# Delta-rule stage of a two-block stack: where the loads of inverted blocks are issued, and when the block levels begin

## The chip, the cores and the metric

The kernel runs on one core of a Trainium2 chip. The metric is device microseconds of one execution. TensorE (PE in the profile) multiplies, VectorE is DVE, ScalarE is ACT, GpSimd is POOL, SyncE is SP. SP, ACT and POOL can issue DMAs; an engine's instructions are taken in the order of its program, DMA issues among them, and an instruction that waits for a semaphore holds what stands behind it on that engine.

## The reference, cut to what matters

The program is a whole small network on 256 tokens of width 1024: a first block (two SwiGLU layers around an mLSTM mixer) and a second block of two layers, a gated delta rule and a sliding-window attention, each followed by a convolution-gated MLP. The change touches the delta rule alone. Its heart, for chunks of 64 tokens and 16 heads:

```
m     = where(strict, einsum('bnhcd,bnhsd->bnhcs', k_beta, k) * decay, 0)
t_mat = triangular_solve(m + eye, eye, lower=True, unit_diagonal=True)   # an inverse for every head and chunk
u     = einsum('bnhcs,bnhse->bnhce', t_mat, v_beta)
w     = einsum('bnhcs,bnhsd->bnhcd', t_mat, k_beta * exp(gc)[..., None])
# then a scan over chunks, a norm, a gate silu(z), and the output product with w_out
```

## The kernel before, in words

**Products.** Every large product streams its weights: `load_half` (L158) issues one DMA of 512 KB from SP into a buffer `raw` (four of them, L163), ACT casts it in two pieces to `whi` (L171), DVE subtracts to get `wlo` (L173), and `mm3` (L247) does three matmuls per tile, the "triple" (L250 to L252). One half holds eight tiles, which is one projection of the delta rule (eight triples, 24 matmuls). There are five pairs of split buffers, so a half's cast waits for the end of the projection five before its own. `wtile` (L194) loads a half when the products three halves earlier are emitted (`LOOK = 3`).

**The delta rule (L719 to L1181).** The chunks are taken as 128 by 128 matrices, four for each of the eight key heads `q8` (32 in all). `stage1` builds them, `ustore` (L966) writes them to HBM as `ud`. `invert(hf)` (L991) reads the 32 by 32 diagonal blocks of four heads `q8` and inverts them on POOL by forward substitution (L1001, L1006, 31 rounds); POOL then copies the result (L1007) and stores it as `xyd[hf]` (L1008). The two inversions, `hf` 0 and 1, follow one another on POOL. `levels(q8)` (L1015) then builds the inverse of the 128 by 128 matrix from its blocks: it loads the matrix again as two tiles `u` (L1018), loads the inverted blocks into a tile `XY` with four DMAs of 32 KB (L1032), and multiplies level by level (L1046, L1056, L1059, L1070, L1075). `solve` and `outp` follow with the head's own products and norm, up to the transposes of L1135. `u`, `r32`, `r64`, the outputs and more share 55 buffers called `u1k`.

**The order.** A planner, `Weave`, decides in which order the instructions are emitted. Fillers (projections of v, q, z, then the output product `op_all`) are taken a triple at a time, and each advances the planner's clock by 0.32; chains (norms, `stage1`, `invert`, `levels`) are generators that yield a cost and a latency. `invert` yields until the planner's estimate of POOL's end (`fill.pool`, L1009) plus 6.0 (L1010), and then marks `("i", hf)`, on which `levels` of four heads wait. `levels(3)` to `levels(5)` wait besides for the end of the head three before. `levels` yields 3.0 between the loads of `XY` and its first product.

**What the compiler makes of it.** The emission order is a priority. The framework's scheduler places each engine's instructions by its own estimate of when their inputs are there, and inserts the semaphores. `after(first, then)` (L144) adds an edge that this scheduler keeps and that puts no wait on the chip. Two such edges stand here: the loads of `XY` are placed after the weight load emitted last (`lastw`, L1035), and the first product of a level is placed after the product emitted last (`lastmm`, L1048).

Of the kernel before, what the change touches and what calls it, by code (L numbers as in the profile page):

```python
# [120 lines left out]
def stack_kernel(ctx, tc, w, xt, cols, rows, gw, baw, rel, kc, kb, out):  # L121
    nc = tc.nc
# [12 lines left out]
    def ps_mm(tag=None):  # L135
        if tag is None:
            rot[0] += 1
            tag = "st" if rot[0] % 3 == 0 else "mm"
        return pp.tile([128, 512], F32, name=tag, tag=tag, bufs=2 if tag == "st" else 4)
# [4 lines left out]
    def after(first, then):  # L144
        tc.add_manual_dep(then.ins, first.ins.name,
                          mybir.DependencyInfo(mybir.DependencyClass.NoSync, mybir.DependencyReason.DATA),
                          reason="order")

    lastw, lastmm = [None], [None]
# [569 lines left out]
    with tc.tile_pool(name="gd", bufs=1) as gp, tc.tile_pool(name="gw", bufs=2) as gq:  # L719
        def unit():  # L720
            return gp.tile([128, SEQ], F32, name="u1k", tag="u1k", bufs=55)
# [24 lines left out]
        fill = Weave(pe=0.32, dve=0.14)  # L746
# [159 lines left out]
        def urows(g):  # L906
            t = ud[g // 16]
            return bass.AP(tensor=t.tensor, offset=t.offset + (g % 16) * UG, ap=[[128, 128], [UG, 2], [1, 128]])
# [82 lines left out]
        def invert(hf):  # L991
            p0 = 64 * hf
            pr = slice(p0, p0 + 64)
            X, Y = Z[pr, :, :, 0], Z[pr, :, :, 1]
            nc.gpsimd.dma_start(out=B[pr], in_=bass.AP(tensor=ud[hf].tensor, offset=ud[hf].offset,
                                                     ap=[[129 * 32, 64], [128, 32], [1, 32]]))
            first = None
            for i in range(31):
                n = 31 - i
                t = tmp[pr, 0:n * (i + 1)].rearrange("p (r j) -> p r j", r=n)  # L1000
                ins = P_.tensor_tensor(out=t, in0=X[:, i, 0:i + 1].unsqueeze(1).to_broadcast([64, n, i + 1]),  # L1001
                                 in1=B[pr, i, i + 1:32].unsqueeze(2).to_broadcast([64, n, i + 1]), op=ALU.mult)
                if first is None and lastinv[0] is not None:
                    after(lastinv[0], ins)
                first = ins
                P_.tensor_tensor(out=X[:, i + 1:32, 0:i + 1], in0=X[:, i + 1:32, 0:i + 1], in1=t, op=ALU.add)  # L1006
            lastinv[0] = P_.tensor_copy(Y, X.rearrange("p i j -> p j i"))  # L1007
            nc.gpsimd.dma_start(out=xyd[hf], in_=Z[pr].rearrange("p a b t -> p a (b t)"))  # L1008
            fill.pool = max(fill.pool, fill.now + 6.0) + INVERT_COST  # L1009
            yield 0.0, fill.pool + 6.0 - fill.now, 0.0  # L1010
            fill.mark("i", hf)

        turn = [0.0]
# [1 line left out]
        def levels(q8):  # L1015
            u = [unit(), unit()]
            for j in range(2):
                nc.sync.dma_start(out=u[j], in_=urows(4 * q8 + 2 * j))  # L1018
            t = max(fill.now, turn[0])
            turn[0] = t + 5.0  # L1020
            yield 0.0, t - fill.now, 0.0
            if q8 < 6:
                XY = xyt[q8 % 3]
            elif q8 == 6:
                XY = gp.tile([128, 4, 256], F32, name="XY", tag="B")
                P_.memset(XY, 0.0)
            else:
                XY = gp.tile([128, 2048], F32, name="XY", tag="Z")[:, 0:1024].rearrange("p (g c) -> p g c", g=4)
                P_.memset(XY, 0.0)
            src = xyd[q8 // 4]  # L1030
            for a in range(4):
                ins = nc.sync.dma_start(out=XY[32 * a:32 * a + 32, :, 64 * a:64 * a + 64], in_=bass.AP(  # L1032
                    tensor=src.tensor, offset=src.offset + (16 * (q8 % 4) + a) * 2048,
                    ap=[[64, 32], [4 * 2048, 4], [1, 64]]))
                after(lastw[0], ins)  # L1035
            xyv = XY.rearrange("p g (c t) -> p g c t", t=2)
            X, Y = xyv[:, :, :, 0], xyv[:, :, :, 1]
            yield 0.0, 3.0, 0.0
            def us(g, r0, nr, c0, ncl):
                return u[g // 2][r0:r0 + nr, (g % 2) * 128 + c0:(g % 2) * 128 + c0 + ncl]  # L1040

            r32 = unit()[:, 0:128].rearrange("p (g n) -> p g n", g=4)
            pr = ps_mm("mm")
            for b in (0, 64):
                for g in range(4):
                    ins = T_.matmul(pr[b + 32:b + 64, g * 32:g * 32 + 32], us(g, b, 32, b + 32, 32), X[b:b + 32, g, b:b + 32],  # L1046
                                    start=True, stop=True)
                    if b == 0 and g == 0:  # L1048
                        after(lastmm[0], ins)
            for b in (32, 96):  # L1050
                S.copy(r32[b:b + 32], pr[b:b + 32, 0:128].rearrange("p (g n) -> p g n", g=4))
            yield 0.5, 0.9, 0.0
            px = ps_mm("mm")
            for b in (0, 64):
                for g in range(4):
                    T_.matmul(px[b:b + 32, g * 32:g * 32 + 32], r32[b + 32:b + 64, g, :],  # L1056
                              Y[b + 32:b + 64, g, b + 32:b + 64], start=True, stop=True)
                for g in range(4 if b == 0 else 0):
                    T_.matmul(px[b + 32:b + 64, g * 32:g * 32 + 32], Y[b + 32:b + 64, g, b + 32:b + 64],  # L1059
                              r32[b + 32:b + 64, g, :], start=True, stop=True)  # L1060
            for b in (0, 64):
                V.tensor_copy(Y[b:b + 32, :, b + 32:b + 64], px[b:b + 32, 0:128].rearrange("p (g n) -> p g n", g=4))
                if b == 0:
                    V.tensor_copy(X[32:64, :, 0:32], px[32:64, 0:128].rearrange("p (g n) -> p g n", g=4))
            yield 1.0, 0.4, 0.8

            r64 = unit().rearrange("p (g n) -> p g n", g=4)
            pr = ps_mm("mm")
            for g in range(4):
                T_.matmul(pr[64:128, g * 64:g * 64 + 64], us(g, 0, 64, 64, 64), X[0:64, g, 0:64], start=True, stop=True)  # L1070
            S.copy(r64[64:128], pr[64:128, 0:256].rearrange("p (g n) -> p g n", g=4))
            yield 0.43, 0.7, 0.0
            px = ps_mm("mm")
            for g in range(4):
                T_.matmul(px[0:64, g * 64:g * 64 + 64], r64[64:128, g, :], Y[64:128, g, 64:128], start=True, stop=True)  # L1075
            V.tensor_copy(Y[0:64, :, 64:128], px[0:64, 0:256].rearrange("p (g n) -> p g n", g=4))
            yield 0.43, 0.4, 0.3
            yield from solve(q8, Y)

        def solve(q8, Y):  # L1080
            n21 = N21.pop(q8)
            pcs = [unit(), unit()]
            pc = [pcs[g // 2][:, (g % 2) * 128:(g % 2) * 128 + 128] for g in range(4)]
            fill.need(("v", 2 * q8))
            fill.need(("v", 2 * q8 + 1))
            pw = ps_mm("mm")
            for j in range(2):
                vh = 2 * q8 + j
                T_.matmul(pw[:, j * 128:j * 128 + 128], Y[:, 2 * j], Vn[:, 0, vh, :], start=True, stop=True)
                S.activation(out=pc[2 * j], in_=pw[:, j * 128:j * 128 + 128], func=AF.Copy,  # L1090
                             scale=cc[:, 0, vh:vh + 1])
            yield 0.43, 1.0, 0.0
            pw2 = ps_mm("mm")
            for j in range(2):
                T_.matmul(pw2[:, j * 128:j * 128 + 128], n21[:, j * 128:j * 128 + 128], pc[2 * j],
                          start=True, stop=True)
            V.tensor_tensor(out=Vn[:, 1, 2 * q8:2 * q8 + 2, :], in0=Vn[:, 1, 2 * q8:2 * q8 + 2, :],
                            in1=pw2[:, 0:256].rearrange("p (a b) -> p a b", a=2), op=ALU.subtract)
            yield 0.43, 0.4, 0.34
            pw3 = ps_mm("mm")  # L1100
            for j in range(2):
                vh = 2 * q8 + j
                T_.matmul(pw3[:, j * 128:j * 128 + 128], Y[:, 2 * j + 1], Vn[:, 1, vh, :], start=True, stop=True)
                S.activation(out=pc[2 * j + 1], in_=pw3[:, j * 128:j * 128 + 128], func=AF.Copy,
                             scale=cc[:, 1, vh:vh + 1])
            yield 0.43, 1.0, 0.0
            yield from outp(q8, pc)
# [352 lines left out]
```

## Time and profile before

| | us |
|---|---|
| median of 3 runs (1329.46 to 1331.79) | 1330.91 |
| the profiled execution | 1331.48 |
| its span, first to last instruction | 1329.7 |

The profiled execution lies 0.57 us above the median. Busy shares of the span: PE 97%, PEld (weight load, overlaps PE) 94%, DVE 71%, ACT 59%, POOL 9%. The granted clock of TensorE has two levels, 2.4 GHz (shown as 1.00) and 1.2 GHz (0.50); over the whole span it was 0.988 in the mean. The delta rule runs from about 547 to 861 us. In the tables below a wait is written in brackets behind the instruction that ended it: [5.16 <-DVE gy L760] says that the engine was idle for 5.16 us before this instruction and that a result of L760 on DVE ended the idle time.

### The profile page before, as it was taken

The page shows a single profiled execution, that of the slowest core. Times are in us where ns is not written, and L with a number is a line of the kernel's source. Part 1 is how long each engine was busy: PE and PEld are TensorE (multiplying, and loading weights), DVE is VectorE, ACT ScalarE, POOL GpSimd, SP SyncE. Part 2 cuts the span into 40 slices and gives each one's busy share as a digit, 9 for nine tenths or more (in the row PEclk, how much of TensorE's full clock was granted, in tenths as well). Part 3 has the DMA queues.
Part 4 walks back from the last instruction along what each step waited for, and adds up shares of the span by engine and source line. Part 5 has one row for each costly group of instructions (what it writes and reads, how often), then busy time and mean ns, then how long its engine had stood idle before and what let it go on. Part 6 is the DMA issues. An engine that isn't in the chain of part 4 may idle for free.

```text
span 1329.7 us, 27373 instructions
## 1 busy us (share of the span) xinstructions
PE 1290.5 (97%) x10665; PEld 1252.4 (94%) x10665; DVE 940.2 (71%) x1856; ACT 788.3 (59%) x1823; POOL 123.6 (9%) x191
## 2 busy tenths in 40 slices
PE   8999999999999999999998799999999999999997
PEld 8999999988999999899997798999999989999997
DVE  7866546776777754588885765798886686998851
ACT  6554445665765554466655555777765676776641
POOL 0000000000000000101879400001100000000000
PEclk9999999999999999999998799999999999999999
DMA  7755553542465655235364352368975532476540
GB/s 258 241 175 175 176 170 112 165 147 72 154 206 183 188 189 169 75 96 183 120 204 153 84 163 80 104 171 233 236 218 197 181 102 69 158 237 191 190 159 33
DMA packets 70306, 213.38 MB, mean 160 GB/s; under 512 B 12517, under 2 KB 19205, under 8 KB 70048
## 3 DMA queue, kind: packets, MB, share of 16 engines
q1 hardware_dynamic: 65264, 204.36, 48.5%
q0 software_dynamic: 2304, 5.43, 2.0%
q10 hardware_dynamic: 2608, 1.84, 0.4%
q8 instruction: 84, 1.38, 0.4%
q14 instruction: 46, 0.38, 0.1%
HBM read 207.00 MB, written 4.59 MB: 159 GB/s over the span
## 4 chain that ended last, share of the span: by engine, by line
PE 77%; POOL 7%; DVE 5%; DMA 4%; ACT 3%; issue 3%; SPq 0%; DVEq 0%; POOLq 0%; ACTq 0%
PE mm L250 12%; PE mm L252 12%; PE mm L251 12%; PE st L251 7%; PE st L252 7%; PE st L250 7%; POOL Z L1006 3%; POOL tmp L1001 3%; DMA raw<-in_w 2%; PE mm L268 2%; PE mm L270 2%; PE mm L272 2%; DVE wlo L173 2%; PE st L268 1%; PE st L272 1%
## 5 line engine op out<-in xcount | busy, mean ns | idle before, releaser
L171 ACT CAST whi<-raw 128x512 fp32r<-128x512 f32 x752 | 439.5, 617 | 332.3 <-PE mm L251 115.0
L173 DVE TENSOR_TENSOR wlo<-raw,whi 128x1024 fp32r<-128x1024 f32 (+1 forms) x377 | 462.6, 1228 | 138.6 <-ACT whi L171 131.2
L250 PE MATMUL mm<-xh,whi 128*128 128x256 f32 (+1 forms) x1040 | 295.2, 284 | 0.0
L252 PE MATMUL mm<-xh,wlo 128*128 128x256 f32 (+1 forms) x1040 | 294.5, 283 | 0.5 <-DVE wlo L173 0.5
L251 PE MATMUL mm<-xl,whi 128*128 128x256 f32 (+1 forms) x1040 | 294.1, 283 | 0.0
L250 PE MATMUL st<-xh,whi 128*128 128x256 f32 (+1 forms) x720 | 207.8, 289 | 1.1 <-DVE u1k L920 1.1
L251 PE MATMUL st<-xl,whi 128*128 128x256 f32 (+1 forms) x720 | 206.7, 287 | 0.0
L252 PE MATMUL st<-xh,wlo 128*128 128x256 f32 (+1 forms) x720 | 206.1, 286 | 0.1
L252 PEld LDWEIGHTS mm<-xh,wlo 128*128 128x128 f32 x1040 | 196.0, 188 | 0.9 <-DVE wlo L173 0.7
L251 PEld LDWEIGHTS mm<-xl,whi 128*128 128x128 f32 x1040 | 195.8, 188 | 0.7 <-DVE xl L380 0.6
L250 PEld LDWEIGHTS mm<-xh,whi 128*128 128x128 f32 x1040 | 196.0, 189 | 0.5 <-DVE fu L428 0.2
L250 PEld LDWEIGHTS st<-xh,whi 128*128 128x128 f32 x720 | 137.8, 191 | 2.8 <-DVE u1k L920 1.3
L252 PEld LDWEIGHTS st<-xh,wlo 128*128 128x128 f32 x720 | 137.9, 192 | 0.4 <-DVE wlo L173 0.3
L251 PEld LDWEIGHTS st<-xl,whi 128*128 128x128 f32 x720 | 137.7, 191 | 0.1
L250 PE MATMUL mm<-hh,whi 128*128 128x256 f32 (+1 forms) x352 | 99.5, 283 | 0.0
L251 PE MATMUL mm<-hl,whi 128*128 128x256 f32 (+1 forms) x352 | 99.4, 282 | 0.0
L252 PE MATMUL mm<-hh,wlo 128*128 128x256 f32 (+1 forms) x352 | 99.4, 282 | 0.0
L250 PEld LDWEIGHTS mm<-hh,whi 128*128 128x128 f32 x352 | 67.0, 190 | 0.0
L251 PEld LDWEIGHTS mm<-hl,whi 128*128 128x128 f32 x352 | 66.5, 189 | 0.0
L252 PEld LDWEIGHTS mm<-hh,wlo 128*128 128x128 f32 x352 | 66.5, 189 | 0.0
L439 DVE SCALAR_TENSOR_TENSOR fu<-mm,colt,fu 128x255 f32<-128x255 f32 x108 | 51.1, 477 | 13.1 <-ACT fu L436 12.9
L250 PE MATMUL st<-hh,whi 128*128 128x256 f32 (+1 forms) x176 | 49.7, 282 | 0.0
(487 smaller groups left out, 2685.9 us busy)
## 6 DMA issues: line engine op xcount, KB each, us to landing
raw<-in_w SPq DMA_DIRECT2D x377, 512.0 KB, 4.0
u1k<-ud SPq DMA_DIRECT2D x16, 128.0 KB, 3.8
Tb<-bvd POOLq DMA_DIRECT2D x16, 128.0 KB, 6.1
gx<-in_w SPq DMA_DIRECT2D x2, 512.0 KB, 5.5
ud<-u1k POOLq DMA_DIRECT2D x8, 128.0 KB, 3.1
ud<-u1k ACTq DMA_DIRECT2D x8, 128.0 KB, 2.5
xyd<-Z POOLq DMA_DIRECT2D x2, 512.0 KB, 4.2
XY<-xyd SPq DMA_DIRECT2D x32, 32.0 KB, 3.4
```

Source lines behind the costliest of these rows:

```text
L171: S.copy(hi[:, c[0]:c[1]], raw[:, c[0]:c[1]])
L173: V.tensor_tensor(out=lo[:, c[0]:c[1]], in0=raw[:, c[0]:c[1]], in1=hi[:, c[0]:c[1]].bitcast(F32), op=ALU.subtract)
L250: T_.matmul(ps, hi, xhh, start=first, stop=False)
L251: T_.matmul(ps, hi, xll, start=False, stop=False)
L252: lastmm[0] = T_.matmul(ps, lo, xhh, start=False, stop=last)
L268: T_.matmul(pss[j], wts[j][0], xhh, start=(k == 0), stop=False)
L270: T_.matmul(pss[j], wts[j][1], xhh, start=False, stop=False)
L272: T_.matmul(pss[j], wts[j][0], xll, start=False, stop=(k == kt - 1))
L439: V.scalar_tensor_tensor(out=t[:, d:], in0=ps[:, :T - d], scalar=wc(2 - d), in1=t[:, d:], op0=ALU.mult, op1=ALU.add)
L1001: ins = P_.tensor_tensor(out=t, in0=X[:, i, 0:i + 1].unsqueeze(1).to_broadcast([64, n, i + 1]), in1=B[pr, i, i + 1:32].unsqueeze(2).to_bro ...
L1006: P_.tensor_tensor(out=X[:, i + 1:32, 0:i + 1], in0=X[:, i + 1:32, 0:i + 1], in1=t, op=ALU.add)
```

## The change

The four DMAs that load the inverted blocks of a head are issued from ACT instead of SP. They keep the edge to the weight load emitted last, which now runs from an instruction on SP to one on ACT, and get a second edge, to the product emitted last on PE. The planner marks an inversion as done 2.0 later on its clock (8.0 instead of 6.0 behind POOL's estimated end).

```
             fill.pool = max(fill.pool, fill.now + 6.0) + INVERT_COST
-            yield 0.0, fill.pool + 6.0 - fill.now, 0.0
+            yield 0.0, fill.pool + 8.0 - fill.now, 0.0
             fill.mark("i", hf)
...
             for a in range(4):
-                ins = nc.sync.dma_start(out=XY[32 * a:32 * a + 32, :, 64 * a:64 * a + 64], in_=bass.AP(
+                ins = nc.scalar.dma_start(out=XY[32 * a:32 * a + 32, :, 64 * a:64 * a + 64], in_=bass.AP(
                     tensor=src.tensor, offset=src.offset + (16 * (q8 % 4) + a) * 2048,
                     ap=[[64, 32], [4 * 2048, 4], [1, 64]]))
                 after(lastw[0], ins)
+                after(lastmm[0], ins)
```

## Rows read from the trace of the kernel before

**Rows 1.** Page, busy time of each engine: us, share of the span, instructions.

```profile
PE 1290.5 (97%) x10665; PEld 1252.4 (94%) x10665; DVE 940.2 (71%) x1856; ACT 788.3 (59%) x1823; POOL 123.6 (9%) x191
```

**Rows 2.** Stretches: length, busy us (instructions) per engine, granted clock, DMA share, GB/s.

```profile
690.00:790.00 100.00, 86.84 (x802) 80.79 (x801) 67.59 (x170) 57.13 (x174) 45.32 (x67) 0.90 0.46 131
697.95:703.11 5.16, 0.00 (x1) 0.00 (x0) 0.99 (x3) 1.80 (x4) 4.31 (x11) 0.70 1.00 323
703.11:706.80 3.69, 3.69 (x17) 3.69 (x18) 2.30 (x5) 2.10 (x6) 3.38 (x5) 0.50 0.72 203
...
755.95:764.90 8.95, 8.95 (x70) 8.31 (x70) 1.33 (x5) 3.28 (x11) 0.00 (x0) 0.50 0.28 76
820.00:850.00 30.00, 26.37 (x203) 24.57 (x203) 17.41 (x53) 16.03 (x52) 0.00 (x0) 0.94 0.32 105
```

**Rows 3.** PE in order of time, 690 to 704: start, us, line, operation, [idle before].

```profile
691.52 0.44 PE L810 MATMUL ax<-kct,gy 128*128 128x128 f32 x2 [1.10 <-DVE gy L760]
...
692.73 0.28 PE L250 MATMUL st<-xh,whi 128*128 128x256 f32 x1
...
695.93 0.28 PE L250 MATMUL ax<-xh,whi 128*128 128x256 f32 x1
...
697.67 0.28 PE L250 MATMUL ax<-xh,whi 128*128 128x256 f32 x1
703.11 0.69 PE L810 MATMUL ax<-kct,gy 128*128 128x128 f32 x2 [5.16 <-DVE gy L760]
```

**Rows 4.** ACT in order of time, 692 to 702.

```profile
692.81 0.62 ACT L171 CAST whi<-raw 128x512 fp32r<-128x512 f32 x1 [0.19 <-PE st L251]
...
701.10 0.62 ACT L171 CAST whi<-raw 128x512 fp32r<-128x512 f32 x1 [5.29 <-DMA raw<-in_w]
```

**Rows 5.** SP's DMA issues in order of time, 682 to 775.

```profile
682.31 0.41 SPq L163 DMA_DIRECT2D raw<-in_w  x1
693.67 2.44 SPq L1032 DMA_DIRECT2D XY<-xyd  x4
696.21 0.38 SPq L1018 DMA_DIRECT2D u1k<-ud  x1
696.68 0.89 SPq L163 DMA_DIRECT2D raw<-in_w  x2
...
738.72 0.35 SPq L163 DMA_DIRECT2D raw<-in_w  x1
749.43 1.73 SPq L1032 DMA_DIRECT2D XY<-xyd  x4
751.27 0.37 SPq L163 DMA_DIRECT2D raw<-in_w  x1
751.75 0.90 SPq L1018 DMA_DIRECT2D u1k<-ud  x2
```

**Rows 6.** SP's waits, first 682 to 694, then 737 to 750: total, times, longest.

```profile
SPq L1032 <- DMA xyd<-Z: 10.3, 1, 10.3
...
SPq L1032 <- DMA xyd<-Z: 10.9, 1, 10.9
```

**Rows 7.** PE in order of time, 737 to 769, with the second stop.

```profile
739.60 0.33 PE L1135 MATMUL mm<-kct,u1k 128*128 128x128 f32 x1 [1.77 <-ACT u1k L1131]
...
755.95 0.39 PE L1046 MATMUL mm<-XY,u1k 32*32 32x32 f32 x4 [4.01 <-DMA u1k<-ud]
...
768.40 0.28 PE L250 MATMUL st<-u1k,whi 128*128 128x256 f32 x1
```

**Rows 8.** Chain of waits, 735 to 782: start, us, what.

```profile
745.20 4.18 DMA xyd<-Z
...
751.75 4.07 DMA u1k<-ud
```

**Rows 9.** DVE and ACT in order of time, 746 to 764.

```profile
746.62 1.22 DVE L173 TENSOR_TENSOR wlo<-raw,whi 128x1024 fp32r<-128x1024 f32 x1
...
763.79 0.62 ACT L171 CAST whi<-raw 128x512 fp32r<-128x512 f32 x1 [1.81 <-PE st L251]
```

**Rows 10.** PE: first products of the levels of head 0, and of head 4.

```profile
708.44 0.59 PE L1046 MATMUL mm<-XY,u1k 32*32 32x32 f32 x16
...
782.22 0.52 PE L1046 MATMUL mm<-XY,u1k 32*32 32x32 f32 x14
```

**Rows 11.** Lines L1032 and L967: issue ns min/median/max, landing after issue in us.

```profile
L1032 SPq DMA_DIRECT2D XY<-xyd x32: 302/423/1117, 693.7 to 770.2; - x32
DMA to landing us min/median/max: 1.7/3.4/5.1
...
L967 ACTq DMA_DIRECT2D ud<-u1k x8: 366/367/395, 644.6 to 666.1; - x8
...
DMA to landing us min/median/max: 1.8/2.7/4.5
```

More of the change, by code (lines that the diff above doesn't have):

```diff
@@ L1009, in invert @@
             fill.pool = max(fill.pool, fill.now + 6.0) + INVERT_COST
-            yield 0.0, fill.pool + 6.0 - fill.now, 0.0
+            yield 0.0, fill.pool + 8.0 - fill.now, 0.0
             fill.mark("i", hf)
@@ L1031, in levels @@
             for a in range(4):
-                ins = nc.sync.dma_start(out=XY[32 * a:32 * a + 32, :, 64 * a:64 * a + 64], in_=bass.AP(
+                ins = nc.scalar.dma_start(out=XY[32 * a:32 * a + 32, :, 64 * a:64 * a + 64], in_=bass.AP(
                     tensor=src.tensor, offset=src.offset + (16 * (q8 % 4) + a) * 2048,
@@ L1035, in levels @@
                 after(lastw[0], ins)
+                after(lastmm[0], ins)
             xyv = XY.rearrange("p g (c t) -> p g c t", t=2)
```

## The prediction

> **What bounds the kernel now.** The busy shares come first: PE is busy for 1290.5 of 1329.7 us [rows 1], so a change off PE counts only where it ends or begins a stop of PE. Next I cut the stage into stretches. Over the 100 us around the block levels (690 to 790) PE is busy for 86.84 us only, at a mean clock of 0.90, while ACT, with 57.13, and the DMA engines, at a share of 0.46, have room [rows 2]. So something holds PE there. PE in order of time shows what: one stop of 5.16 us before 703.11 [rows 3] and one of 4.01 before 755.95 [rows 7], each followed by a stretch at 1.2 GHz, 703.11 to 706.80 and 755.95 to 764.90, in which PE never rests [rows 2].
>
> Both stops lead to SP. The first: PE waits for L760, which stands behind ACT's cast at 701.10, and that cast waited 5.29 us for weights [rows 4]. The weights were issued at 696.68, and the load before them at 682.31; between the two, SP stood at the first load of inverted blocks until 693.67 [rows 5], for 10.3 us, because POOL's blocks had not yet landed in HBM [rows 6]. The second: SP stands for 10.9 us in the same way before 749.43 [rows 5, 6], and the two `u` tiles of head 3, which have nothing to do with it, go out behind that at 751.75 and land 4.07 us later [rows 8], when PE begins.
>
> **The change part by part.**
>
> *SP loses 32 issues and both holds.* After 682.31 the next weights go out as soon as a `raw` buffer is free; the cast at 692.81 already waits for a split buffer and not for a load [rows 4], so with weights at hand the next cast comes with the end of the projection at 695.9 [rows 3], five us earlier, and the 5.16 us go. The slow stretch behind it goes with the stop: 3.5 us at half rate, worth 1.75. At the second stop the weights of 751.27 must still wait for the subtraction that ends at 746.62 + 1.22 = 747.84 [rows 9]; the `u` tiles then go out at about 748.3 and land at 752.4, 0.4 us after PE gets there at 751.94. So 3.6 of the 4.0 us go. The 1.10 us stop at 690.4 left the clock at full rate: the two transposes and eight matmuls behind it take 1.21 us, from 691.52 to 692.73 [rows 3], while one matmul alone takes 0.21 in the slow stretch (17 in 3.69 us [rows 2]). So a rest of 0.4 should cost no rate, and I let the whole slow stretch go here too: 8.95 us at half rate, worth 4.4. Sum of what goes: 5.2 + 1.75 + 3.6 + 4.4 = 14.9 us. If the cover fails, that is if something else is as late as the held load, each stop comes back at its own price.
>
> *ACT gets 32 issues, and the same wait.* Where they land on ACT decides. The edges put no wait on the chip, they only place the loads. The load at 682.31 is the one emitted last before the block loads. By the cast order it feeds the half cast at 692.81, and that cast waits for the projection that ends at 692.6, so it is used five projections after that one. The product emitted last belongs to the half three before it, the second projection after 692.6: those begin at 692.73 and 695.93 [rows 3], so it is the one from 695.93. The planner's extra 2.0 is six triples more at 0.32, some 2.2 us of PE at the 0.355 us per triple of this stretch (24 matmuls and two transposes from 692.73 to 695.93 [rows 3], less the transposes). So ACT meets the loads of head 0 when PE is at about 699 to 701, with the stop gone, and the blocks have landed by 693.67 [rows 5]: 5 us of margin, no wait. Likewise for head 4: the load of 738.72 is cast at 763.79 behind the end of a projection [rows 9], three halves less brings the projection that begins at 768.40 [rows 7], 19 us behind the landing at 749.4 [rows 8], and still 4 us if all 14.9 us come off. Behind a block load on ACT stand the casts and the PSUM evacuations that PE needs within a projection; they would be held as SP's loads are now.
>
> *The issue time on ACT.* No row shows these loads on ACT. The nearest, stores from ACT, take 0.367 us each, and the loads on SP 0.423 [rows 11]: 32 of them are 11.7 to 13.5 us, in a stretch where ACT is 57% busy [rows 2]. The bounds in PE time are 0 and 13.5; I take 1.5, nearer the lower one, since four in a row are 1.5 us and ACT's work has to be late by more than its slack to reach PE.
>
> *Blocks that come later.* The first product of head 0, at 708.44 [rows 10], stands at least 3.0 of planner time, nine triples or 3.2 us of PE, behind the loads. From ACT the loads take 4 x 0.367 us of issue and 1.8 to 4.5, in the middle 2.7 us of landing [rows 11]: 3.3 to 6.0, in the middle 4.2. So PE may stand for 0.1 to 2.8 us at each of heads 0, 1 and 2, 0.3 to 8.4 in all; other heads' products between load and use shorten that, and the scheduler may place more fillers ahead, so the lower bound is 0. I take 1.5. Heads 4 to 7 use their blocks late for another reason (782.22 [rows 10], after `u` tiles), so nothing is added there.
>
> *Levels that begin 2.0 later.* While there are fillers, PE does other work meanwhile. At the end there are none: from 820 to 850 PE is busy for 26.37 of 30 us [rows 2]. The bounds are a loss of 2.0, and a gain of 1.8 if the stop at L1135 [rows 7] falls away because its head moves. I take a loss of 1.0.
>
> The Trainium skill, page "DMA: Bandwidth & Descriptors", section "Issuing engines are not separate DMA queues", speaks against the change: DMAs issued from SP, ACT and GpSimd share the same 16 DMA engines, and issuing from several saves only the issue time, which is usually small. By that rule alone SP would save some 13 us of issues that nobody waits for, and the time would stay. The rows disagree about the size, as what SP loses here is a hold of 10.3 and 10.9 us [rows 6].
>
> **The sum.** 14.9 - 1.5 - 1.5 - 1.0 = 10.9 us. From the profiled execution's own 1331.48 us that is 1320.6; the profiled run lies 0.6 above the median of the runs shown, which makes 1320.0. I predict 1320.5. Its own range, with the costs between 0 and about 9 and up to 1.8 of gain, is 1315 to 1326.
>
> **The rivals.**
>
> *Only the first stop goes.* The `u` tiles of head 3 may be late because they wait for a `u1k` buffer of head 0, whose levels now begin later. For: they stand behind the held load in SP's order, so the trace can't show when their buffer came free. Against: SP issued them at once when its turn came. Then 6.9 us go and the costs of 4.0 stay: 1328.6.
>
> *The stop moves to another transfer.* While PE stood in the first stop, the DMA engines were busy throughout, at 323 GB/s [rows 2]; if the weights are late for lack of transfer time, they stay late on any queue. Against: the share over 690 to 790 is 0.46, and the burst is what had been held back. Then the gain covers no more than its costs: 1331.
>
> *ACT is held instead of SP (slower).* The edges place by the scheduler's estimate; on SP that estimate was too early by 10.3 and 10.9 us [rows 6]. If ACT reaches the loads before the blocks have landed, its casts and evacuations stop. This decides from the point at which ACT gets there before 693.6 or 749.4. SP's hold cost PE half its length, as loads run ahead; ACT's work runs ahead by one projection, some 3.2 us, so a hold of 10.3 would stop PE for 7 us, with 3 to 4 more at 1.2 GHz: about 10.5 each, 21 in place of the 15 of now, and the time 1337. Against: the product edge, which gives 5 us of margin. In the same page's section "Anatomy of one DMA — SWDGE (gpsimd) path" the Trainium skill says that a DMA's semaphore wait takes place on the issuing sequencer before dispatch; SP's waits [rows 6] agree, and on ACT it would be the same. Nor can the product edge fail harmlessly: if it doesn't move the loads, this is the case that comes.
>
> **How the numbers follow.** What a measurement of this kernel can tell from no change is about 0.2%, 2.7 us. The forecast gets 0.60, the rival with one stop 0.17, the moved transfer 0.10, ACT held 0.13. Faster: 0.60 and most of the second, 0.73; same: 0.14; slower: 0.13. The range reaches from the ceiling (14.9 and 1.8 of gain, 1314) to where the moved transfer ends, 1331; outside it lie ACT held and a little of the rest.
>
> **What would show it.** Right: on SP no wait for xyd is left; a cast directly after 695.9; no stop of PE over 2 us between 695 and 760, with the clock at 1.00 there; ACT's block loads issued without a wait, the first at about 699 to 701, with PE's waits before L1046 under 2 us each; PE busy for about 95 of the 100 us from 690 on. Wrong: ACT idle for several us in front of its first block load, a stop at L1046 of more than 3 us with the clock at 0.50 behind it, or the end of the stage, 820 to 850, longer by what was won.

## The result, and the profile after

The changed kernel takes 1338.2 us (median of 5 runs, 1337.15 to 1340.78) against 1331.02 for the kernel before beside it: ratio 1.0059, 95% interval 1.0042 to 1.0076. It is slower, 7.2 us by the medians, and outside the predicted range.

The mechanism that was forecast works in the main. The first page line after, then the block loads (duration in ns, minimum, median, maximum; first and last start; landing in us), the longest waits of PE from 640 to 870 (total, times, longest), the first product of head 0, and the stretch from 690 to 790 as in [rows 2], all of the changed kernel. Lines behind the edit are one higher there: L1047 is L1046 of before.

```profile
PE 1297.9 (97%) x10665; PEld 1257.5 (94%) x10665; DVE 942.5 (71%) x1856; ACT 787.9 (59%) x1823; POOL 124.8 (9%) x191
```

```profile
L1032 ACTq DMA_DIRECT2D XY<-xyd x32: 309/325/815, 696.8 to 782.5; - x32
...
DMA to landing us min/median/max: 1.6/2.8/5.1
```

```profile
PE ax L810 <- DVE gy L760: 4.8, 2, 3.7
PE mm L1136 <- ACT u1k L1132: 3.8, 5, 1.8
```

```profile
701.39 0.41 PE L1047 MATMUL mm<-XY,u1k 32*32 32x32 f32 x8 [0.71 <-POOL Z L1006]
```

```profile
690.00:790.00 100.00, 90.03 (x846) 83.22 (x844) 69.43 (x166) 57.75 (x173) 44.67 (x67) 0.97 0.44 124
```

The stops of 5.16 and 4.01 us [rows 3, 7] are gone, the loads cost ACT less than they cost SP (0.325 against 0.423 us each [rows 11]), and head 0 begins at 701.39 where it began at 708.44 [rows 10]. What is left is one stop of 3.7 us, at 747.32, again at L810 behind L760; so PE is busy for 90.03 of the 100 us from 690 on, where about 95 were named as a sign, at a clock of 0.97. Yet the stage ends later.

To see where, single executions are laid over one another on a **common scale**: a "triple" is the three matmuls L250 to L252, and each trace is shifted so that its 1300th triple is at 665.0 (the changed kernel by +2.31, the kernel before by -0.75). The 1620th triple, the 36th of the product behind the delta rule, then marks the end of the stage. Five stretches of that scale, 665 to 700, 740, 785, 820 and the end, first of the kernel before, then after (length, busy us of PE, PEld, DVE, ACT, POOL, granted clock, DMA share, GB/s):

```profile
665.75:700.75 35.00, 31.03 (x258) 30.14 (x256) 27.56 (x42) 18.36 (x42) 25.88 (x36) 0.99 0.71 211
700.75:740.75 40.00, 35.87 (x373) 33.02 (x374) 27.89 (x67) 24.77 (x78) 36.08 (x51) 0.92 0.37 116
740.75:785.75 45.00, 39.86 (x322) 37.37 (x321) 30.13 (x87) 26.19 (x81) 5.33 (x7) 0.85 0.45 128
785.75:820.75 35.00, 34.78 (x398) 31.54 (x396) 20.57 (x61) 17.98 (x56) 0.00 (x0) 1.00 0.32 99
820.75:878.10 57.35, 53.72 (x431) 51.29 (x430) 44.05 (x114) 41.87 (x108) 2.19 (x4) 0.97 0.38 113
```

```profile
662.69:697.69 35.00, 33.91 (x284) 33.12 (x282) 30.55 (x46) 22.14 (x51) 25.99 (x29) 1.00 0.78 237
697.69:737.69 40.00, 37.14 (x377) 33.76 (x376) 26.96 (x62) 21.59 (x71) 35.52 (x56) 0.96 0.27 81
737.69:782.69 45.00, 39.86 (x340) 37.41 (x339) 31.82 (x87) 25.77 (x79) 8.04 (x10) 0.96 0.43 124
782.69:817.69 35.00, 30.50 (x285) 26.13 (x284) 14.80 (x39) 14.28 (x44) 0.00 (x0) 0.71 0.40 121
817.69:881.41 63.72, 60.06 (x500) 57.10 (x499) 48.63 (x133) 45.02 (x122) 2.18 (x4) 0.97 0.33 98
```

Read each line as a loss: length less PE's busy time is idle, and busy time times (1 - clock) is what the clock takes. Before, the first three stretches lose 4.3, 7.0 and 11.1 us, together 22.4; after, 1.1, 4.3 and 6.7, together 12.2. **So 10.2 us are won by 785.** The fourth stretch loses 0.2 before and 13.3 after (4.5 idle, and 30.50 x 0.29 = 8.8 of clock), the last 5.2 and 5.5. The stage is 6.4 us longer: 3.2 by these losses, and 3.2 in what is left, PE's busy time counted at full clock, which this account can't split.

What fills that fourth stretch is seen at its start: PE in order of time, changed kernel, where head 4 begins.

```profile
785.08 0.28 PE L250 MATMUL st<-u1k,whi 128*128 128x256 f32 x1
...
785.42 0.28 PE L250 MATMUL st<-u1k,whi 128*128 128x256 f32 x1
786.59 0.28 PE L1047 MATMUL mm<-XY,u1k 32*32 32x32 f32 x4 [0.89 <-issue]
786.79 0.39 PE L251 MATMUL st<-u1k,whi 128*128 128x256 f32 x1
```

The products (fillers) do run ahead: triple 1519 comes at 811.2 before and 790.7 after, on the common scale. But head 4 starts at 788.9 instead of 781.5. From 791 on there are no fillers left (the next, the second half of the output product, needs head 4), and four heads run their small products alone, at a clock of 0.71. Counted in PE's program, head 4's first product stands behind triple 1481 before and behind triple 1516 after.

### The profile page after: what moved, and what is told of

Its sections match the earlier page's. It is cut to its first block, busy times and chain, and to the rows that moved or that the text cites. A ratio compares the mean times of both kernels' runs of the same rounds, so it can differ in the third digit from the quotient of the medians.

```text
span 1336.0 us, 27362 instructions
## 1 busy us (share of the span) xinstructions
PE 1297.9 (97%) x10665; PEld 1257.5 (94%) x10665; DVE 942.5 (71%) x1856; ACT 787.9 (59%) x1823; POOL 124.8 (9%) x191
## 4 chain that ended last, share of the span: by engine, by line
PE 75%; DVE 9%; DMA 5%; POOL 4%; ACT 3%; issue 3%; SPq 0%; DVEq 0%; ACTq 0%; POOLq 0%
PE mm L250 12%; PE mm L252 11%; PE mm L251 11%; PE st L251 6%; PE st L250 6%; PE st L252 6%; DMA raw<-in_w 4%; DVE wlo L173 3%; POOL Z L1006 2%; PE mm L270 2%; PE mm L272 2%; PE mm L268 2%; POOL tmp L1001 2%; PE st L268 1%; PE st L272 1%
## 5 line engine op out<-in xcount | busy, mean ns | idle before, releaser
L250 PE MATMUL mm<-xh,whi 128*128 128x256 f32 (+1 forms) x1040 | 296.3, 285 | 2.1 <-DVE fu L439 2.1
L252 PE MATMUL mm<-xh,wlo 128*128 128x256 f32 (+1 forms) x1040 | 295.6, 284 | 0.0
L250 PE MATMUL st<-xh,whi 128*128 128x256 f32 (+1 forms) x720 | 205.5, 285 | 1.1 <-DVE u1k L920 1.1
L252 PE MATMUL st<-xh,wlo 128*128 128x256 f32 (+1 forms) x720 | 204.2, 284 | 0.3 <-DVE wlo L173 0.2
L250 PEld LDWEIGHTS mm<-xh,whi 128*128 128x128 f32 x1040 | 197.0, 190 | 2.5 <-ACT fu L436 2.2
L252 PEld LDWEIGHTS mm<-xh,wlo 128*128 128x128 f32 x1040 | 197.0, 189 | 0.4 <-DVE wlo L173 0.2
L250 PEld LDWEIGHTS st<-xh,whi 128*128 128x128 f32 x720 | 136.0, 189 | 2.7 <-DVE u1k L920 1.3
L252 PEld LDWEIGHTS st<-xh,wlo 128*128 128x128 f32 x720 | 136.0, 189 | 0.9 <-DVE wlo L173 0.7
L250 PE MATMUL mm<-hh,whi 128*128 128x256 f32 (+1 forms) x352 | 99.6, 283 | 0.0
L252 PE MATMUL mm<-hh,wlo 128*128 128x256 f32 (+1 forms) x352 | 99.5, 283 | 0.0
L250 PEld LDWEIGHTS mm<-hh,whi 128*128 128x128 f32 x352 | 67.1, 191 | 0.0
L252 PEld LDWEIGHTS mm<-hh,wlo 128*128 128x128 f32 x352 | 66.6, 189 | 0.0
L252 PE MATMUL st<-hh,wlo 128*128 128x256 f32 (+1 forms) x176 | 49.8, 283 | 0.0
```

Source lines behind the costliest of these rows:

```text
L250: T_.matmul(ps, hi, xhh, start=first, stop=False)
L252: lastmm[0] = T_.matmul(ps, lo, xhh, start=False, stop=last)
```

## The experiments

The expectations use the common scale and these counts. In the table, places are the number of triples ahead of the first product of head 3 and of head 4 in PE's program, counted in each trace; losses are worked out from one profiled execution each as above; the ratio is to the kernel before on the same chip.

| kernel | places 3, 4 | loss to 785 | 785 to 820 | behind 820 | median us | ratio, interval |
|---|---|---|---|---|---|---|
| before | 1442, 1481 | 22.4 | 0.2 | 5.2 | 1331.0 | |
| after | 1465, 1516 | 12.2 | 13.3 | 5.5 | 1338.2 | 1.0059, 1.0042 to 1.0076 |
| e1_queue6 | 1446, 1494 | 11.7 | 5.8 | 5.3 | 1331.3 | 0.9991, 0.9967 to 1.0015 |
| e2_sp_late8 | 1448, 1517 | 13.3 | 11.0 | 5.4 | 1338.6 | 1.0041, 1.0016 to 1.0065 |
| e3_queue10 | 1446, 1486 | 13.4 | 4.5 | 4.1 | 1330.2 | 0.9988, 0.9963 to 1.0012 |
| e4_second_early | 1446, 1468 | 22.7 | 0.5 | 0.0 | 1324.7 | 0.9930, 0.9901 to 0.9960 |
| e5_own_u | 1449, 1504 | 14.8 | 11.6 | 6.0 | 1335.3 | 1.0037, 1.0009 to 1.0065 |
| e6_sp_edge | 1445, 1499 | 16.4 | 6.0 | 5.0 | 1329.3 | 0.9986, 0.9962 to 1.0010 |
| e7_no_edge | 1439, 1490 | 18.8 | 5.9 | 3.3 | 1331.2 | 1.0010, 0.9989 to 1.0030 |
| e8_own_u_early | 1444, 1457 | 20.5 | 9.5 | 0.4 | 1333.3 | 1.0010, 0.9984 to 1.0036 |
| e9_first_late | 1465, 1504 | 13.1 | 7.7 | 4.9 | 1332.3 | 1.0005, 0.9982 to 1.0029 |
| e10_second_late | 1446, 1499 | 8.6 | 7.2 | 3.6 | 1330.6 | 1.0000, 0.9982 to 1.0018 |
| e11_sp_early | 1438, 1469 | 25.4 | 0.8 | 0.3 | 1328.9 | 0.9993, 0.9975 to 1.0010 |
| e12_second_4 | 1446, 1482 | 20.1 | 6.3 | 0.3 | 1330.8 | 1.0004, 0.9986 to 1.0023 |
| e13_u_pool | 1465, 1516 | 13.9 | 11.0 | 5.4 | 1338.6 | 1.0044, 1.0025 to 1.0062 |
| e14_early_u_pool | 1446, 1468 | 11.5 | 0.3 | 0.0 | 1324.5 | 0.9940, 0.9917 to 0.9962 |
| e15_second_early_again | 1446, 1468 | 21.3 | 0.5 | 0.0 | 1323.2 | 0.9932, 0.9906 to 0.9958 |
| e16_place4 | 1465, 1476 | 22.0 | 3.1 | 1.3 | 1337.1 | 1.0048, 1.0028 to 1.0068 |
| e17_place4to7 | 1465, 1476 | 23.2 | 12.2 | 0.7 | 1345.3 | 1.0107, 1.0079 to 1.0136 |
| e18_place34 | 1430, 1476 | 23.1 | 0.5 | 1.1 | 1329.0 | 0.9989, 0.9968 to 1.0009 |

**Which part of the change costs: the queue or the 2.0?** `e1_queue6` is the change with 6.0, `e2_sp_late8` the kernel before with 8.0, `e3_queue10` the change with 10.0.

```
e1  -  yield 0.0, fill.pool + 8.0 - fill.now, 0.0    +  ... + 6.0 ...   (from the changed kernel)
e2  -  yield 0.0, fill.pool + 6.0 - fill.now, 0.0    +  ... + 8.0 ...   (from the kernel before)
e3  -  yield 0.0, fill.pool + 8.0 - fill.now, 0.0    +  ... + 10.0 ...  (from the changed kernel)
```

> The change with 6.0 in place of 8.0: block loads on ACT behind the product edge, levels begun as before. Cover theory: the two stops go and give PE about 14 us, but that time goes to fillers, and what counts is how many filler triples are left behind the first product of head 4 (the fillers end at triple 1520, where the output product needs head 4). Here it stands behind triple 1494, before at 1481, in the change at 1516. Against before that is 14 us won and 13 triples of 0.355 us (4.6 us) of cover lost: about 1322 us, between 1318 and 1327. Issue theory (32 DMA issues on ACT, or blocks that land later from there, delay the heads): about as the change, 1335 to 1338 us. Later-begin theory (each us of planner time at the start of a level is a us of the time): 2 us less than the change, 1336 us.

> The kernel before with 8.0 in place of 6.0: block loads stay on SP, levels begin later. Cover theory: in PE's program head 4's first product stands behind triple 1517, with 3 filler triples left, and both holds of SP stay: 36 triples (12.8 us) of cover less than before, about 5 us more at 1.2 GHz, the holds a little shorter: about 1345 us, between 1338 and 1349. Issue theory: as before, 1331 us, since nothing moves to ACT. Later-begin theory: 1333 us.

> The change with 10.0 in place of 8.0. In PE's program the first product of head 0 comes 5 triples later than in the change, but that of head 4 stands behind triple 1486 instead of 1516, since the scheduler places it elsewhere. Cover theory: 30 triples more of cover than the change and no holds: about 1321 us, between 1316 and 1327. Later-begin theory: 2 us slower than the change, 1340 us. Issue theory: as the change, 1338 us.

The queue alone gives no time (e1, 1331.3). 8.0 costs with the loads on SP as well (e2). So the cost of issuing on ACT is out as the cause: it is there in e1 and e3, and not in e2. But 10.0 costs nothing that can be told, so it is not a price per us of delay either. The cover theory (the time goes by the fillers left behind head 4's first product) was too large in e1 and e3 and at the edge of its range in e2; the later-begin theory missed all three.

**Does the chain of heads set the end?** `e4_second_early` lets the second inversion's heads begin earlier.

```
-  yield 0.0, fill.pool + 8.0 - fill.now, 0.0
+  yield 0.0, fill.pool + (6.0 if hf == 0 else -6.0) - fill.now, 0.0
```

> The change with 6.0 for the first inversion and -6.0 for the second: heads 4 to 7 are emitted 12 to 14 of planner time earlier. In PE's program head 4 begins behind triple 1468, with 52 fillers left, and the last transposes of heads 4 to 7 stand at 1504, 1519, 1535 and 1542. Cover theory: 14 us won at the stops and the idle time at the end of the stage shortened: 1314 to 1319 us. If ACT now meets the block loads of head 4 before they have landed (749.4 us in the trace of before), ACT is held for the difference, some 3 us or less, and the time is a few us longer. Issue theory: 1335 to 1338 us.

1324.7, faster than both kernels, though short of the 1314 to 1319 expected.

**Do the shared `u1k` buffers or the held queue delay head 4?** `e5_own_u` is the change with buffers of their own for the `u` tiles; `e6_sp_edge` is the kernel before with the product edge added to SP's loads; `e7_no_edge` has the loads on ACT without that edge and with 6.0; `e8_own_u_early` is e5 with the second inversion at -9.0.

```
e5  -  u = [unit(), unit()]
    +  u = [gp.tile([128, SEQ], F32, name="lu", tag="lu", bufs=4) for _ in range(2)]   # and u1k: bufs=51
e6  +  after(lastmm[0], ins)     (only this; loads on SP, 6.0)
e7  -  ins = nc.sync.dma_start(out=XY[...], ...)   +  ins = nc.scalar.dma_start(...)   (only this)
e8  e5 and  + (6.0 if hf == 0 else -9.0)
```

> The change with the u tiles of the levels in four buffers of their own (51 instead of 55 left for the rest), all else as in the change. Chain theory: the stage ends some 37 us behind the last transposes of head 7, those come some 58 us behind the first product of head 4, and that one waits for the later of two things: the u tiles of head 4 and the last transposes of head 3. In the change the u tiles decide (landed 7 to 8 us behind the transposes of head 3, since SP issues them behind weight loads). With own buffers they are there early, head 4 begins behind the transposes of head 3: 6 to 8 us less than the change, 1330 to 1332 us. Rival (begin 2.0 later, or loads on ACT, cost by themselves): 1337 to 1339 us as the change.

> The kernel before with the product edge added: block loads stay on SP, levels begin as before. The edge puts them four weight loads further back in SP's program, so SP should no longer be held at them. Chain theory: as the queue-and-edge kernel with 6.0 (first product of head 4 behind triple 1499, there 1494): within 3 us of that kernel and of before, 1328 to 1333 us, though both stops of PE go. Issue theory in what is left of it (32 issues on ACT cost a few us): 3 to 5 us faster than that kernel, 1325 to 1327 us.

> Block loads on ACT without the product edge, levels begun as before (6.0). In ACT's program the first load of blocks stands four halves earlier, so ACT reaches it before the blocks have landed and is held there, and again at head 4's. PE-bound theory (a stop of PE is paid in full): stops of 5 to 8 us at each hold, with slow clock behind: 1336 to 1340 us. Chain theory: the holds stop PE, but what they take is filler time of which the end of the stage has some to spare; the heads go on as the blocks land: 1329 to 1334 us, though PE stops for longer than in the queue-and-edge kernel.

> The change with own buffers for u and 6.0 for the first inversion, -9.0 for the second. In PE's program head 4 begins behind triple 1457 and the last transposes of head 7 stand at 1521 instead of 1557. Chain theory: head 4 begins as soon as its blocks have landed and head 3 is through, some 10 us earlier than with -6.0 alone; the fillers then last to the end, and PE bounds the stage: 1314 to 1320 us. If ACT is held at head 4's blocks (they land at about 751 us), the gain is some 3 us less. Issue theory: no faster than the kernel with -6.0, 1325 us.

e5 and e8 missed. In e6 SP waits for `xyd` no longer than 0.5 us, and the time is not told apart from e1's: against the hold the queue need not be moved, the edge does it. PE's second stop stays in e6 all the same, at head 3's `u` tiles:

```profile
753.50 0.31 PE L1047 MATMUL mm<-XY,u1k 32*32 32x32 f32 x4 [4.40 <-DMA u1k<-ud]
```

e7 is the most telling: its waits (of ACT, then of PE, as total, times, longest) show the third rival of the prediction at the blocks of the first inversion; at those of the second ACT is not held.

```profile
ACT Vn L812 <- DMA xyd<-Z: 11.0, 1, 11.0
```

```profile
PE ax L810 <- DVE gy L760: 11.8, 3, 9.6
```

ACT is held 11.0 us and PE stops for 9.6, and the time is 1331.2, as in e1, where ACT is not held and PE's longest stop is 3.0. **A stop of PE of that size costs nothing here that these runs can tell** (the two intervals, up to 1.0015 and 1.0030, overlap). That fits products with slack, and the table agrees: e10 loses least ahead of 785 (8.6) and takes 1330.6, e4 loses 22.7 there and takes 1324.7. In e8 the heads are too early: they run without fillers between them (clock 0.50 over 785 to 800), and the products are left over at the end.

**Which 2.0, and is the queue needed for e4's gain?**

```
e9   + (8.0 if hf == 0 else 6.0)      (from the changed kernel)
e10  + (6.0 if hf == 0 else 8.0)      (from the changed kernel)
e11  + (6.0 if hf == 0 else -6.0)     (from the kernel before: loads on SP, no product edge)
e12  + (6.0 if hf == 0 else -4.0)     (from the changed kernel)
```

> The change with 8.0 behind the first inversion and 6.0 behind the second. In program order head 3's first product stands behind triple 1465 as in the changed kernel (1446 with 6.0 twice) and head 4's behind 1504 (1494 with 6.0 twice, 1516 in the changed kernel). If the loss comes from the heads of the first inversion (head 3 late, so head 4 late): 1335 to 1338 us. Rival, the loss comes from the heads of the second inversion alone: 1331 us as with 6.0 twice.

> The change with 6.0 behind the first inversion and 8.0 behind the second. Head 3's first product stands behind triple 1446, head 4's behind 1499. If the loss comes from the first inversion's heads: 1330 to 1333 us. Rival, the second inversion's 2.0: 1336 to 1338 us.

> The kernel before with the loads of the blocks left on SP, and -6.0 instead of 6.0 behind the second inversion. Chain theory: head 4's first product stands behind triple 1469 instead of 1481, so the end of the stage comes 3 to 4 us earlier although SP is held for the second store some 11 us or longer: 1326 to 1329 us. Rival, SP's wait is what costs and the queue has to be moved first: 1331 to 1337 us.

> The change with 6.0 behind the first inversion and -4.0 behind the second. Head 4's first product stands behind triple 1482, the last head's transposes behind 1554 (1542 with -6.0, where the products were left over at the end). Balance theory (the later of heads and products sets the end): 1323 to 1325 us, at or below the 1324.7 with -6.0. Rival, only head 4's start counts: 1326 to 1328 us, between -6.0 and 6.0.

Neither 2.0 alone costs anything that can be told; both together do. Nothing in the expectations foresaw that. e11, which has e4's -6.0 but neither the queue nor the product edge, lies within its interval of no change, and that interval, from 0.9975, lies above e4's, which ends at 0.9960. So most of e4's gain needs the queue or the edge; which of the two isn't settled. e12 missed both theories: its head 4 stands at 1482, one triple behind that of the kernel before, and its time is that kernel's.

**SP's queue once more, or the place in PE's program?** e9 and the changed kernel keep within 2 us of one another up to head 4. There the changed kernel's `u` loads go out 6.7 us later on the common scale, behind three weight loads that wait for buffers. SP's issues, and its longest wait, changed kernel:

```profile
769.10 12.87 SPq L163 DMA_DIRECT2D raw<-in_w  x3
782.07 5.50 SPq L1018 DMA_DIRECT2D u1k<-ud  x8
```

```profile
SPq L163 <- DVE u1k L391: 18.7, 2, 11.4
```

That looks like the cause. `e13_u_pool` takes these eight loads off SP; PE's program is unchanged at the heads' first products. e14 does the same in e4, and e15 is e4 again.

```
-  nc.sync.dma_start(out=u[j], in_=urows(4 * q8 + 2 * j))
+  (nc.sync if q8 < 4 else nc.gpsimd).dma_start(out=u[j], in_=urows(4 * q8 + 2 * j))
```

> The changed kernel, with the eight u loads of heads 4 to 7 issued from POOL, whose program is done by then, instead of SP, where in the changed kernel they stand behind three weight loads that wait for raw buffers. PE's program order at the heads' first products is the changed kernel's (1396, 1407, 1419, 1465, 1516, 1520, 1520, 1520). SP theory: the tiles of head 4 land before 783 us on the common scale (789.4 in the changed kernel), its first product comes with the last transposes of head 3 at 782 to 783, the stage ends 6 us earlier than in the changed kernel, and the time is 1331 to 1333 us. Rival, the place of head 4 in the program order alone sets it: head 4 at 788 or later, 1337 to 1339 us.

> The change with 6.0 and -6.0 (the fastest run so far) and the u loads of heads 4 to 7 on POOL. Its stage ended with products left over, not with the heads: 1323 to 1326 us by that, no gain. Rival, head 4 still waits for its u tiles (landed 773.2, first product 776.2): 1320 to 1322 us.

> The change with 6.0 and -6.0 once more, beside the other two on one chip: 1323 to 1326 us if its gain over the kernel before (ratio 0.993) is the kernel's; 1328 to 1331 us if most of it was one build's or one chip's.

It is not the cause. POOL's issues and PE in order of time, e13:

```profile
766.78 0.75 POOL L1018 DMA_DIRECT2D u1k<-ud  x1 [15.45 <-PE mm L1136]
767.81 5.04 POOL L1018 DMA_DIRECT2D u1k<-ud  x7 [0.28 <-PE mm L1076]
```

```profile
787.23 0.28 PE L252 MATMUL st<-u1k,wlo 128*128 128x256 f32 x1
787.34 0.28 PE L250 MATMUL st<-u1k,whi 128*128 128x256 f32 x1
787.54 0.31 PE L1047 MATMUL mm<-XY,u1k 32*32 32x32 f32 x4
```

On the common scale the first `u` load goes out 16.0 us earlier, at 768.4, and its tiles land by 771.9, its blocks by 765.6; yet its product begins at 787.54 (789.2 on the common scale), with products in front of it and no wait: PE has simply not come to it. The Trainium skill, page "PSUM — Partial Sum Buffer", section "Engine vs sequencer instructions", says that matmuls start and complete in program order; these rows agree. e15 repeats e4's gain; e14 adds nothing to it.

**The place alone.** The planner emits head 4's first product behind triple 1467 before and 1476 after; the framework's scheduler places it behind 1481 and 1516. `e16_place4` holds it at 1476 by edges to every product emitted later, on top of e13; `e17_place4to7` holds heads 4 to 7, `e18_place34` heads 3 and 4. The edges move the heads behind as well: heads 5 to 7, at 1520 in e13, stand at 1487, 1493 and 1506 in e16 and in e18, and at 1486, 1491 and 1496 in e17.

```
 def mm3(ps, wt, x, first, last):
-    T_.matmul(ps, hi, xhh, start=first, stop=False)
+    ins = T_.matmul(ps, hi, xhh, start=first, stop=False)
+    if headmm[0] is not None:
+        after(headmm[0], ins)
...
                         after(lastmm[0], ins)
+                        if q8 == 4:              # e17: q8 >= 4, e18: q8 in (3, 4)
+                            headmm[0] = ins
```

> e13_u_pool with one more set of edges: every product emitted behind head 4's first product is also placed behind it, so that PE's program has it where it is emitted, behind triple 1476, and not where the framework's scheduler puts it, behind 1516. Order theory: PE passes triple 1476 at 768 to 770 us on the common scale, the tiles of head 4 land at 766 to 772, so its first product comes by 777 (789.2 in e13_u_pool), the stage ends 6 to 10 us earlier, and the time is 1327 to 1332 us. Rival, head 4 waits for something else that also comes late: its first product stays behind 785, and the time at 1336 to 1339 us.

> The same with heads 4 to 7 all held at their emitted places (1476, 1486, 1491, 1496 instead of 1516, 1520, 1520, 1520). If the chain of heads sets the end: 1325 to 1330 us. Rival: the products are left over behind the heads as in e8_own_u_early, and the gain is 0 to 3 us against e16_place4.

> The same with heads 3 and 4 at their emitted places (1430 and 1476 instead of 1465 and 1516). Head 3 earlier makes its transposes earlier, which stand ahead of head 4's first product: 1326 to 1331 us, 0 to 2 us under e16_place4. Rival: PE stops at triple 1430 for head 3's tiles, whose loads land at 733.6 and 760.4 in e13_u_pool, for more than 5 us, and the time is above that of e16_place4.

e16 missed. PE in order of time, e16, where head 4 begins (L1140 are the transposes, L1049 the first product):

```profile
777.12 0.64 PE L1122 MATMUL mm<-u1k 128*128 128x128 f32 x2
782.43 1.25 PE L1140 MATMUL mm<-kct,u1k 128*128 128x128 f32 x4 [4.68 <-ACT u1k L1136]
783.61 0.42 PE L1049 MATMUL mm<-XY,u1k 32*32 32x32 f32 x4
```

Held at 1476, head 4 comes to stand right behind the last transposes of head 3, and those are late because head 3 itself stands at 1465 where it is emitted behind 1430. PE waits 4.68 us for it, and the loss moves from 785 to 820 (11.0, now 3.1) to ahead of 785 (13.9, now 22.0). With head 3 in its place as well, e18 is at 1329.0: its interval, 0.9968 to 1.0009, lies wholly below those of e13, 1.0025 to 1.0062, and of e16, 1.0028 to 1.0068. e18 and e13 differ in these edges alone, e18 and e16 in the place of head 3 alone (the first products of the other heads stand at the same triples). So **the places of the heads in PE's program are what the 7 us hang on**; the 2.0, the queue and the issue cost are the same in all three. What the edges move on the other engines with them isn't separated. PE's stops are no help here: e18 has one of 7.17 us, longer than any of e13's (3.4), and is faster.

```profile
746.73 0.48 PE L1140 MATMUL mm<-kct,u1k 128*128 128x128 f32 x1 [7.17 <-ACT u1k L1136]
```

No single place orders the times. Of the kernels without held fillers, those with head 4 at 1481 to 1499 take 1329.3 to 1331.3 us and those with it at 1516 or 1517 take 1338.2 to 1338.6; but e9 has head 3 as late as the changed kernel and takes 1332.3, e16 has head 4 early and takes 1337.1, and e17, with heads 3 and 4 where e16 has them, takes 1345.3. Nor does the start of head 4 tell it: on the common scale it comes at 782.4 in e18 and at 783.4 in e16, and the rest of the gain comes behind it, where from 785 to 800 e16 has a clock of 0.78 and e18 one of 1.00; e16, then e18:

```profile
785.24:800.24 15.00, 15.00 (x155) 13.47 (x154) 4.49 (x11) 4.18 (x12) 0.00 (x0) 0.78 0.20 54
783.10:798.10 15.00, 15.00 (x170) 13.27 (x164) 4.71 (x11) 4.42 (x13) 0.00 (x0) 1.00 0.45 129
```

The last three stretches of e18, then of e15 (columns as above):

```profile
738.10:783.10 45.00, 35.73 (x307) 32.73 (x307) 31.42 (x86) 25.00 (x79) 13.21 (x19) 0.80 0.39 116
783.10:818.10 35.00, 34.51 (x378) 31.22 (x372) 19.11 (x58) 17.80 (x57) 0.00 (x0) 1.00 0.39 116
818.10:873.48 55.38, 54.32 (x456) 52.50 (x456) 44.68 (x113) 42.15 (x106) 2.18 (x4) 1.00 0.44 122
```

```profile
739.05:784.05 45.00, 38.29 (x355) 35.06 (x355) 27.47 (x84) 24.60 (x84) 7.74 (x13) 0.85 0.38 105
784.05:819.05 35.00, 34.53 (x354) 31.94 (x354) 24.15 (x73) 22.01 (x69) 0.00 (x0) 1.00 0.43 130
819.05:871.26 52.21, 52.21 (x433) 50.50 (x433) 44.54 (x110) 40.96 (x104) 2.18 (x4) 1.00 0.45 129
```

In e15 PE is never idle from 819.05 to the end, at full clock, though it lost as much ahead of 785 as the kernel before: fillers last until the heads are done. e17, with fillers held behind all four heads, loses most of all.

## Why the prediction was wrong

*SP loses both holds, 14.9 us.* Right as to PE's stops, wrong as to the end. Both stops went, a new one of 3.7 us came at 747.32, and the losses to 785 fell by 10.2 us. That this lies near the 10.9 of the forecast is chance: 14.9 were to go, and the costs that make 10.9 of it mostly did not show there. **The step that failed is that a stop taken from PE comes off the end.** The prediction asked only what PE waits for there, and not whether the work behind the stop has slack. The products that it delayed now run 10 to 20 us ahead (triple 1480 at 769.9 instead of 780.4, 1519 at 790.7 instead of 811.2 on the common scale), and the end gains nothing by it: without the extra 2.0 the change takes 1331.3 (e1), as the kernel before, and e7 puts a 9.6 us stop back with no loss that can be told. In e1 the losses to 785 fall by 10.7 and those from 785 to 820 rise by 5.6, where head 4 stands 13 triples later than before; how much of the won time was slack, and how much that place took back, no run separates.

*Issue time on ACT, 1.5 (0 to 13.5).* Nothing that can be told: e6 on SP and e1 on ACT differ by 2.0 us, with overlapping intervals.

*Blocks that come later, 1.5.* Wrong sign, if anything: head 0's first product waited 0.71 us, and came 4.0 us earlier on the common scale (7.05 in the traces' own times [rows 10], less the shifts of 2.31 and 0.75).

*Levels that begin 2.0 later, 1.0 (-1.8 to 2.0).* Mis-sized, and the cause of the loss. I read the 2.0 as a delay on the clock. It moves the emission of heads 3 and 4 by 5 and 9 triples (1425 to 1430, 1467 to 1476); in PE's program the change moves them by 23 and 35 (1442 to 1465, 1481 to 1516). Of these 4 and 13 come with the queue and the edge (e1), whose emission is that of before; the scheduler turned the 2.0 into the other 19 and 22, and on SP into 6 and 36 (e2). With 6.0 the same change takes 1331.3, with 8.0 1338.2: some 7 us. The last of the signs named as "wrong", an end of the stage longer by what was won, came true, at 785 to 820 rather than at 820 to 850.

*The rivals.* "Only the first stop goes" did not happen in the change; in e6 the second stop did stay, where SP issues the `u` tiles at 747.35, behind a weight load that had waited 14.2 us for its buffer. "The stop moves to another transfer" did not happen: the new stop at 747.32 ends with a result of VectorE, and ACT waits for no load there. "ACT is held" did not happen in the change, and where it did, in e7, it did not cost the 10.5 us put on it; that its 1337 lies next to the measured 1338.2 is chance.

Left open: why the scheduler places head 4 so late with both 2.0 (1516 on ACT, 1517 on SP) and not with either one or with 10.0; its estimates leave no row in a trace. The account by stretches is of single executions: e14's has a stage of 197.5 us, 10 shorter than e15's, after 8.4 us more ahead of it, while the medians are 1.3 apart, which I can't explain. e1, e3, e10 and e11 have stages 3.1 to 5.8 us shorter than the kernel before and medians that are not told apart from it. The medians, not these stages, carry the conclusions.

## What to carry to other kernels

Before you price a stop of the busiest engine, ask what the work behind it is needed for: where independent work fills the engine between links of a chain, a stop that only delays the filler can be free, as the 9.6 us of e7 were as far as these runs can tell, and taking it away can leave the end of the chain with nothing to run beside it. Count what is left of the filler when the chain ends; the two should run out together. Where a scheduler stands between emission and program, compare the engine's program order before pricing any change of a due time, as here a move of 9 triples became one of 22, on SP of 36.

## What the runs showed of the hardware

Where the heads' small products run with no fillers between them, the granted clock falls although PE looks busy: in the changed kernel its mean is 0.71 over 35 us in which PE is busy for 30.50, and in e8 it is 0.50, which is 1.2 GHz, over 15 us in which PE never rests:

```profile
783.95:798.95 15.00, 15.00 (x125) 13.03 (x123) 7.49 (x22) 6.18 (x22) 0.00 (x0) 0.50 0.23 71
```

Executions of the same instructions can differ in steps: PE's program is the same in all twenty kernels up to triple 1300, yet from triple 600 to 620, at some 300 us, their profiled executions, one of each, took 19.8 to 19.9, 21.4 or 22.9 us, and nothing between. That is why the stage is compared on a scale that begins behind it.
